# Feature-major products that stream both parts of the activations in one 512-column matmul, into two halves of a PSUM bank that are added afterwards

## The chip, the core and the metric

The kernel runs on one core of a Trainium2 chip. The metric is the device time in microseconds (us) of one execution. TensorE (PE in the profile) multiplies, VectorE (DVE) and ScalarE (ACT) evacuate PSUM and do the element-wise work, GpSimd (POOL) does a few small pieces, and SyncE (SP) issues the large loads; ScalarE issues some small ones.

## What is computed

Two transformer blocks over 256 tokens of width 1024, in float32. Cut to what matters:

```python
# first block
h = rmsnorm(x, g_mix);  z = h @ w_in            # x_rnn, g_rnn, q, k, v, gate_a, gate_b
y_a = (rg_lru(conv(x_rnn)) * gelu(g_rnn)) @ w_rnn_proj
y_b = sliding_window_attention(q, k, v) @ w_attn_proj
x = x + (sigmoid(gate_a) * y_a + sigmoid(gate_b) * y_b) @ w_out
x = x + square(relu(rmsnorm(x, g_mlp) @ w_up)) @ w_down      # w_up: 1024 x 4096
x = x + (p @ w_ple_proj) * sigmoid(rmsnorm(x, g_ple) @ w_ple_gate)
# second block
h = h + (g_a * (mla(...) @ w_attn_branch) + g_b * (pool(...) @ w_pool_branch)) @ w_mix_out
h = h + memory_cross_attention(rmsnorm(h), rmsnorm(mem))     # 4 heads of 256, 256 memory rows
h = h + moe(rmsnorm(h))                                      # 32 experts, two for each token
out = rmsnorm(h, final_norm_g)
```

## The kernel before

**Two parts of every operand.** TensorE takes a rounded form of float32 (float32r). So each weight and each activation is kept as a high part (a cast on ScalarE) and the rest (a subtraction on VectorE), made by `split` (L271 to L273), and each product is three matmuls into the same PSUM accumulator, leaving out rest times rest:

```python
def mm3(self, acc, xh, xl, wh, wl, start, stop):     # L304
    mm(acc, xh, wh, start=start, stop=False)         # L306
    mm(acc, xl, wh, start=False, stop=False)         # L307
    mm(acc, xh, wl, start=False, stop=stop)          # L308
```

**Two kinds of products.** `gemm` is token-major: 128 tokens of the activations are the stationary operand and up to 512 columns of weights stream. `gemm_fm` (L330) is feature-major: a block of 128 weight columns is stationary and the 256 tokens stream, so the result has features on the partitions. There the roles of the arguments of `mm3` are exchanged: L306 is high weight by high activation, L307 is the weight's rest by high activation, L308 is high weight by the activation's rest. One block is 8 steps over the 1024 inputs (k) of three matmuls each, 24 matmuls of 256 columns. Its result takes half of a PSUM bank, and a function `evac` reads it from there.

**Where feature-major products stand.** There are 64 such blocks: 16 at the start of the first block (`lru_in`, `gelu_in`, tile `acc`; their evacuation begins on VectorE with a multiplication by the norm's row, L710 and its twin in `gelu_in`), 32 in the MLP's up projection (`mlp`, tile `pt`; ScalarE's relu L860, VectorE's square L862, then a split into the tile `hid`), and 16 in the cross attention (keys and queries, tile `acc`, evacuated by a split). The activations of these products are `State` objects (`st`): for each part a tile of four k-steps by 256 tokens. `trans_split` fills a state four k-steps and 128 tokens at a time, 512 columns for each cast and subtraction.

**The order of the work.** The program is a list of parts. A part is a slice of weights that is split two parts ahead of its use (L272, L273 with the tiles `raw` and `w`), and the matmuls that use it. Background work (attention, recurrence) is advanced a step per part. A scheduler in the tile framework then orders each engine's instructions; each engine runs its own list in order. In the first block's first part the background is sliding-window attention: transposes of probabilities `pr` on TensorE (L464), copied by ScalarE to `pT` (L466), multiplied with the values (L841), heads turned by transposes (L817) that ScalarE casts to `qT` (L819); and the recurrence's gates (L719 on TensorE, L720 on ScalarE).

PSUM has four banks under the name `acc` and four under `pt`. Weights in flight and split weights share one pool of SBUF tiles.

Of the kernel before, what the change touches and what calls it, by code (L numbers as in the profile page):

```python
# [15 lines left out]
ALU = mybir.AluOpType  # L16
# [35 lines left out]
class Raw:  # L52
    """Weights on their way: loaded far ahead, in the order of use."""
# [5 lines left out]
class Part:  # L59
    """A slice of weights, split or as it is, and what runs on it."""  # L60
# [5 lines left out]
class State:  # L66
    """Activations, feature-major, as a float32r part and the exact rest: [128, kt, 256 tokens]."""

    def __init__(self, net, kt=8, early=False):
        self.net, self.kt, self.t = net, kt, {}  # L70
        self.new = net.early if early else net.act
        self.ss, self.r, self.rh = {}, {}, {}
# [5 lines left out]

    def v(self, i, kt, t=None, n=None):
        x = self._tile(i, kt // 4)  # L80
        c = slice(None) if t is None else slice(t * P, (t + 1) * P)
        return x[:, kt % 4, c] if n is None else x[:, kt % 4:kt % 4 + n, c]


class _Late:
    """A state that is made later."""
# [8 lines left out]
class Net:  # L95
# [28 lines left out]
    def early(self, shape, dt=F32, name="e"):  # L124
        """Tiles of the first block's first part only; their room then goes to weights on their way."""
# [36 lines left out]
    def later(self, n, fn):  # L162
        """Runs fn after n more parts."""
# [6 lines left out]
    def manual(self, engines=None):  # L170
        """From here on, the engines take their instructions in the order of the program."""
# [19 lines left out]
    def until(self, gens):  # L191
        """Advances the background until the generators of the list have ended."""
# [82 lines left out]
    def trans_gain(self, src, k0, n, gcol=None):  # L275
        """Transposes of src [128 tokens, n*128], n up to 4, scaled by a gain per feature."""
# [9 lines left out]
    def trans_split(self, srcs, st, k0, n, gcol=None):  # L286
        """Transposes and gains of each block of tokens of srcs, into the split state st."""
        xs = [(t, self.trans_gain(src, k0, n, gcol)) for t, src in srcs]
        for t, x in xs:
            self.split(x, st.v(0, k0, t, n), st.v(1, k0, t, n))  # L290

# [18 lines left out]
    def gemm(self, st, KT, w, c0, n, evac):  # L310
        """Token-major: out[t] = x[t] @ w[:, c0:c0+n]."""
# [18 lines left out]
    def gemm_fm(self, st, KT, w, c0, n, evac, space=None):  # L330
        """Feature-major: out[128 features, 256 tokens] for each block of 128 columns."""
        rs = [(k0, self.rawload(w, k0, min(4, KT - k0), c0, n)) for k0 in range(0, KT, 4)]
        for b in range(n // P):
            def fn(h, l, b=b):
                acc = (space or self.accp)()[:, 0:S]
                for k in range(KT):
                    self.mm3(acc, h[:, k, :], l[:, k, :], st.v(0, k), st.v(1, k), k == 0, k == KT - 1)
                evac(b, acc)
# [1329 lines left out]
```

## Time and profile before

| what | value |
|---|---|
| runs | 996.68, 992.30, 992.56 us; median 992.56 |
| span of the profiled execution | 990.5 us; the median of the runs is 2.06 us above it |
| TensorE busy | 965.8 us (98%) |
| VectorE busy | 555.0 us (56%) |
| ScalarE busy | 498.2 us (50%) |
| feature-major matmuls | 1536 of the 5445 on TensorE |

Busy time is time in which an engine has an instruction in it. Matmuls overlap: the next one starts before the one before it has left the array, so the mean duration of a row is longer than the distance from one start to the next. A clock column (PEclk) gives the granted TensorE clock as a share of full speed, 2.4 GHz.

### The profile page before, as it was taken

To read this page: it belongs to the slowest core of one execution; us is meant where nothing else is said; L and a number is where in the kernel's file an instruction comes from. 1 tells how busy PE (TensorE), PEld (TensorE's weight loads), DVE (VectorE), ACT (ScalarE), POOL (GpSimd) and SP (SyncE) were. 2 spreads that over 40 slices of the span, in tenths; PEclk is the share of its full clock that TensorE was granted. 3 is DMA by queue.
4 is the path that set the end of the run, shared out by engine and by line. 5 is a ranking of instruction groups with operands and counts; after the bars stand their busy time and mean duration, and the time that the engine had idled before them with its cause. 6 is when DMAs were issued, how large, how long until landed. Compare 5 with 4: busy or idle time off the path is not lost.

```text
span 990.5 us, 14266 instructions
## 1 busy us (share of the span) xinstructions
PE 965.8 (98%) x5445; PEld 740.2 (75%) x5445; DVE 555.0 (56%) x1102; ACT 498.2 (50%) x951; POOL 34.6 (3%) x67
## 2 busy tenths in 40 slices
PE   7999999999999999999999999999989999999995
PEld 5889888888999999889887878998854444444442
DVE  5987888777665555577655588664451212212112
ACT  5666799746654444466556646545333222323222
POOL 4200000000000000000100000000000000000000
PEclk9999999999999999999999999999989999999998
DMA  9553245574655555644663544446899999999981
GB/s 296 201 174 125 86 136 173 190 263 163 208 192 201 171 170 178 213 130 170 226 201 128 178 162 170 170 171 218 279 354 354 374 361 375 362 378 361 371 310 45
DMA packets 141317, 222.63 MB, mean 225 GB/s; under 512 B 9522, under 2 KB 79419, under 8 KB 139067
## 3 DMA queue, kind: packets, MB, share of 16 engines
q1 hardware_dynamic: 137552, 218.91, 64.9%
q10 hardware_dynamic: 3691, 2.74, 0.9%
q8 instruction: 45, 0.74, 0.3%
q14 instruction: 29, 0.24, 0.1%
HBM read 220.59 MB, written 1.05 MB: 224 GB/s over the span
## 4 chain that ended last, share of the span: by engine, by line
PE 94%; DVE 2%; ACT 1%; issue 1%; DMA 1%; POOL 0%; SPq 0%; DVEq 0%; POOLq 0%; ACTq 0%
PE acc L308 17%; PE acc L306 17%; PE acc L307 17%; PE pt L1438 11%; PE pt L1459 6%; PE pt L1385 3%; PE acc L1469 3%; PE pt L307 3%; PE pt L308 3%; PE pt L306 3%; PE pt L279 1%; DVE w L273 1%; PE pt L464 1%; PE pt L1039 1%; PE pt L1451 1%
## 5 line engine op out<-in xcount | busy, mean ns | idle before, releaser
L273 DVE TENSOR_TENSOR w<-raw,w 128x512 fp32r<-128x512 f32 (+4 forms) x288 | 273.7, 969 | 114.9 <-ACT w L272 113.2
L272 ACT CAST w<-raw 128x512 fp32r<-128x512 f32 (+4 forms) x288 | 236.3, 847 | 153.8 <-PE acc L308 117.1
L306 PE MATMUL acc<-w,st 128*128 128x512 f32 (+2 forms) x508 | 197.7, 393 | 0.0
L307 PE MATMUL acc<-w,st 128*128 128x512 f32 (+2 forms) x508 | 197.5, 389 | 0.0
L308 PE MATMUL acc<-w,st 128*128 128x512 f32 (+2 forms) x508 | 193.4, 389 | 0.2 <-DVE w L273 0.2
L308 PEld LDWEIGHTS acc<-w,st 128*128 128x128 f32 x508 | 95.8, 189 | 19.0 <-DVE w L273 0.6
L306 PEld LDWEIGHTS acc<-w,st 128*128 128x128 f32 x508 | 95.9, 189 | 18.6 <-ACT st L272 0.5
L307 PEld LDWEIGHTS acc<-w,st 128*128 128x128 f32 x508 | 95.9, 189 | 17.6 <-DVE st L273 0.2
L273 DVE TENSOR_TENSOR y<-pt,y 128x512 fp32r<-128x512 f32 x32 | 22.1, 692 | 109.3 <-ACT y L272 109.3
L1438 PE MATMUL pt<-raw,xg 128*64 128x512 f32 x296 | 83.1, 598 | 0.0
L308 PE MATMUL acc<-st,w 128*128 128x256 f32 x256 | 73.7, 288 | 0.0
L306 PE MATMUL acc<-st,w 128*128 128x256 f32 x256 | 73.5, 287 | 0.0
L307 PE MATMUL pt<-st,w 128*128 128x256 f32 x256 | 72.4, 283 | 1.1 <-DVE w L273 1.1
L307 PE MATMUL acc<-st,w 128*128 128x256 f32 x256 | 73.4, 287 | 0.0
L306 PE MATMUL pt<-st,w 128*128 128x256 f32 x256 | 72.3, 283 | 0.0
L308 PE MATMUL pt<-st,w 128*128 128x256 f32 x256 | 71.8, 283 | 0.0
L1438 PE MATMUL pt<-rawa,xg 128*64 128x512 f32 x216 | 65.1, 598 | 0.0
L1438 PEld LDWEIGHTS pt<-raw,xg 128*64 128x64 f32 x296 | 24.7, 138 | 45.7 <-issue 44.8
L307 PEld LDWEIGHTS pt<-st,w 128*128 128x128 f32 x256 | 49.1, 192 | 1.5 <-DVE w L273 1.3
L306 PE MATMUL acc<-w,hid 128*128 128x512 f32 x128 | 50.0, 390 | 0.0
L307 PE MATMUL acc<-w,hid 128*128 128x512 f32 x128 | 49.9, 390 | 0.0
L308 PE MATMUL acc<-w,hid 128*128 128x512 f32 x128 | 49.8, 389 | 0.0
(361 smaller groups left out, 1460.5 us busy)
## 6 DMA issues: line engine op xcount, KB each, us to landing
raw<-in_w_in_dram SPq DMA_DIRECT2D x31, 1024.0 KB, 5.2
raw<-in_w_exp_gate_dram SPq DMA_DIRECT2D x37, 512.0 KB, 8.5
raw<-in_w_exp_up_dram SPq DMA_DIRECT2D x37, 512.0 KB, 8.7
raw<-in_w_exp_down_dram SPq DMA_DIRECT2D x17, 1024.0 KB, 9.5
raw<-in_w_up_dram SPq DMA_DIRECT2D x16, 1024.0 KB, 5.4
raw<-in_w_down_dram SPq DMA_DIRECT2D x16, 1024.0 KB, 6.8
rawa<-in_w_exp_down_dram SPq DMA_DIRECT2D x30, 512.0 KB, 8.1
rawa<-in_w_exp_gate_dram SPq DMA_DIRECT2D x54, 256.0 KB, 7.7
```

What stands on the lines that cost most here:

```text
L272: self.nc.scalar.copy(h, src)
L273: self.nc.vector.tensor_sub(l, src, h.bitcast(F32))
L279: self.nc.tensor.transpose(p[:, i, :], src[:, i * P:(i + 1) * P], self.ident)
L306: mm(acc, xh, wh, start=start, stop=False)
L307: mm(acc, xl, wh, start=False, stop=False)
L308: mm(acc, xh, wl, start=False, stop=stop)
L464: nc.tensor.transpose(p[:, i, :], pr[:, i, kb * P:(kb + 1) * P], self.ident)
L1039: nc.tensor.matmul(o, V[mb][:, c0:c0 + P], pT[h][:, mb, :], start=mb == 0, stop=mb == 1)
L1385: nc.tensor.matmul(p, xs[t][i][:, k * P:(k + 1) * P], oh[b, t].rearrange("p e s -> p (e s)"), start=n == 0, stop=n == 3)
L1438: nc.tensor.matmul(guP[p][64 * e:64 * e + 64], xg[b, hf][:, k, c0:c0 + 64], gu_of(tiles[e], k), start=kt == 0, stop=kt == 7)
L1459: nc.tensor.matmul(q[64 * e:64 * e + 64], hT[p][:, f, 64 * e:64 * e + 64], d_of(tiles[e], f, c), start=f == 0, stop=f == 1)
L1469: nc.tensor.matmul(acc[t, c], stt[b][:, j, t, :], y[p, c][i], start=False, stop=p == NP - 1 and i == 1)
```

## The change

`gemm_fm` issues two matmuls for each k-step instead of three. The weight's high part meets both parts of the activation at once, side by side, 512 columns into the two halves of one bank; the weight's rest meets the activation's high part, 256 columns, and is added into the first half. (At the last k-step the order of the two is turned round, so that the wide one closes both halves.) After the 16 matmuls ScalarE copies the second half to an SBUF tile `fm`, VectorE adds the first half to it, and `evac` reads `fm` in place of PSUM.

```diff
 class State:
-    def __init__(self, net, kt=8, early=False):
-        self.net, self.kt, self.t = net, kt, {}
+    def __init__(self, net, kt=8, early=False, both=False):
+        self.net, self.kt, self.t, self.both = net, kt, {}, both
...
+    def hl(self, kt):
+
+        if kt // 2 not in self.t:
+            self.t[kt // 2] = self.new([P, 2, 2, S], F32R, name="st")
+        return self.t[kt // 2][:, kt % 2]
+
     def v(self, i, kt, t=None, n=None):
+        c = slice(None) if t is None else slice(t * P, (t + 1) * P)
+        if self.both:
+            x = self.hl(kt)[:, i, c]
+            return x if n is None else self.t[kt // 2][:, kt % 2:kt % 2 + n, i, c]
...
-            self.split(x, st.v(0, k0, t, n), st.v(1, k0, t, n))
...
+            self.split_into(x, st, k0, t, n)
+
+    def split_into(self, x, st, k0, t, n):
+        m = 2 if st.both else n
+        for i in range(0, n, m):
+            self.split(x[:, i:i + m], st.v(0, k0 + i, t, m), st.v(1, k0 + i, t, m))
...
     def gemm_fm(self, st, KT, w, c0, n, evac, space=None):
...
-                acc = (space or self.accp)()[:, 0:S]
+                acc = (space or self.accp)((P, 2, S))
+                mm = self.nc.tensor.matmul
                 for k in range(KT):
-                    self.mm3(acc, h[:, k, :], l[:, k, :], st.v(0, k), st.v(1, k), k == 0, k == KT - 1)
-                evac(b, acc)
+                    last = k == KT - 1
+                    if last:
+                        mm(acc[:, 0], l[:, k, :], st.v(0, k), start=False, stop=False)
+                    mm(acc, h[:, k, :], st.hl(k), start=k == 0, stop=last)
+                    if not last:
+                        mm(acc[:, 0], l[:, k, :], st.v(0, k), start=False, stop=False)
+                s = self.act([P, S], name="fm")
+                self.nc.scalar.copy(s, acc[:, 1])
+                self.nc.vector.tensor_tensor(s, acc[:, 0], s, op=ALU.add)
+                evac(b, s)
...
-            xp = self.act([P, S], name="xp")
+            xp = acc
...
-            x = self.act([P, S], name="gx")
+            x = acc
...
-                r = self.act([P, S], name="r")
-                nc.scalar.activation(r, p, AF.Relu)
                 q = self.act([P, S], name="rq")
-                v.tensor_tensor(q, r, r, op=ALU.mult)
+                v.scalar_tensor_tensor(q, p, 0.0, p, op0=ALU.max, op1=ALU.mult)
```

The states that feed feature-major products (`st0`, the MLP's `st_u`, the cross attention's `st_x` and `st_mem`) are made with `both=True`. Their tiles hold two k-steps with both parts, so they are filled two k-steps at a time: two casts and two subtractions of 256 columns where there was one of 512. `lru_in` and `gelu_in` then work in place on `fm`; in the MLP, relu and square become one VectorE instruction (`scalar_tensor_tensor`), and ScalarE's relu is replaced by its copy.

On TensorE in the first part, where attention and recurrence run beside the feature-major blocks (of the blocks for `gelu_in`), this is before; the transposes L464 stand between the feature-major matmuls:

```order
L306 MATMUL acc<-st,w 128x256
L464 MATMUL pt<-ident,pr 128x128 x2
L307 MATMUL acc<-st,w 128x256
...
L464 MATMUL pt<-ident,pr 128x128 x6
L306 MATMUL acc<-st,w 128x256
...
L719 MATMUL pt<-xc,w_rg 128x256
L719 MATMUL pt<-xc,w_ig 128x256
L841 MATMUL pt<-pT,kv 64x256 x2
L817 MATMUL pt<-ident,qs 128x128 x4
L841 MATMUL pt<-pT,kv 64x256 x4
L817 MATMUL pt<-ident,qs 128x128 x4
```

and this after (L489 was L464, L745 was L719, L867 was L841, L843 was L817):

```order
L356 MATMUL acc<-st,w 128x256
L357 MATMUL acc<-st,w 128x512
L489 MATMUL pt<-ident,pr 128x128 x12
L745 MATMUL pt<-xc,w_rg 128x256
L745 MATMUL pt<-xc,w_ig 128x256
L867 MATMUL pt<-pT,kv 64x256 x2
L843 MATMUL pt<-ident,qs 128x128 x4
L867 MATMUL pt<-pT,kv 64x256 x4
L843 MATMUL pt<-ident,qs 128x128 x4
L745 MATMUL pt<-xc,w_rg 128x256
L745 MATMUL pt<-xc,w_ig 128x256
```

All twelve transposes have moved behind the feature-major matmuls, next to the products that need their copies.

On ScalarE at the same place, this is before (L735 and L737 belong to `gelu_in`, L713 to `lru_in`'s convolution, `st` and `qT` are the attention's output and turned heads):

```order
L713 ACTIVATE xc<-xp,cols 128x256 x3
L272 CAST w<-raw 128x512 x2
L466 COPY pT<-pt 128x512 x3
L272 CAST w<-raw 128x512 x2
L735 ACTIVATE gs<-gx 128x256
L272 CAST w<-raw 128x512 x4
L720 ACTIVATE r<-pt,hbb_rg 128x256
L720 ACTIVATE i<-pt,hbb_ig 128x256
L272 CAST st<-pt 128x2x128
L819 CAST qT<-pt 128x512
```

and this after (L739 was L713, L282 was L272, L491 was L466, L761 was L735, L746 was L720, L845 was L819; L361 is the new copy):

```order
L739 ACTIVATE xc<-fm,cols 128x256 x3
L282 CAST w<-raw 128x512 x6
L491 COPY pT<-pt 128x512 x3
L761 ACTIVATE gs<-fm 128x256
L746 ACTIVATE r<-pt,hbb_rg 128x256
L746 ACTIVATE i<-pt,hbb_ig 128x256
L282 CAST st<-pt 128x2x128
L845 CAST qT<-pt 128x512
L361 COPY fm<-acc 128x256
L282 CAST st<-pt 128x2x128
L845 CAST qT<-pt 128x512
```

The casts of weights that stood between the copies `pT` and the gate `r` now stand ahead of the copies.

On VectorE at the beginning of the MLP, from the instruction that takes the norm's factor (L386, in the change L411) on, this is before. `w_2703` is the weights of the fifth block of the up projection, two halves of 512 columns; `hid` is a split of a finished block:

```order
L386 TENSOR_SCALAR s_2611<-s_2609 128x1
L862 TENSOR_TENSOR rq_2647<-r_2645 128x256
L273 TENSOR_TENSOR w_2703<-raw_2404,w_2703 128x512
L273 TENSOR_TENSOR w_2703<-raw_2450,w_2703 128x512
L273 TENSOR_TENSOR hid_2644<-rq_2647,hid_2643 128x256
L862 TENSOR_TENSOR rq_2683<-r_2681 128x256
```

and this after, where `w_2609` is the fifth block's weights, `w_2761` the eighth's, `w_2794` the first of the down projection, L362 the new addition and L886 relu and square in one:

```order
L411 TENSOR_SCALAR s_2531<-s_2529 128x1
L362 TENSOR_TENSOR fm_2555<-pt_2538,fm_2555 128x256
L886 SCALAR_TENSOR_TENSOR rq_2560<-fm_2555 128x256
L283 TENSOR_TENSOR w_2609<-raw_2316,w_2609 128x512
L283 TENSOR_TENSOR w_2609<-raw_2362,w_2609 128x512
...
L283 TENSOR_TENSOR w_2761<-raw_2316,w_2761 128x512
L283 TENSOR_TENSOR w_2761<-raw_2362,w_2761 128x512
L362 TENSOR_TENSOR fm_2631<-pt_2614,fm_2631 128x256
L960 TENSOR_SCALAR s_2602<-s_2602 128x16
L283 TENSOR_TENSOR w_2794<-raw_2426,w_2794 128x1024
```

One more 256-column instruction stands between the norm's factor and the fifth block's weights.

## Rows read from the trace of the kernel before

**Rows 1.** The page's span, busy time of the engines, and chain by engine.

```profile
span 990.5 us, 14266 instructions
PE 965.8 (98%) x5445; PEld 740.2 (75%) x5445; DVE 555.0 (56%) x1102; ACT 498.2 (50%) x951; POOL 34.6 (3%) x67
PE 94%; DVE 2%; ACT 1%; issue 1%; DMA 1%; POOL 0%; SPq 0%; DVEq 0%; POOLq 0%; ACTq 0%
```

**Rows 2.** Groups by shape: feature-major matmuls, two of six; busy us, mean ns.

```profile
L308 PE MATMUL acc<-st,w 128*128 128x256 f32 x256 | 73.7, 288 | 0.0
L306 PE MATMUL pt<-st,w 128*128 128x256 f32 x256 | 72.3, 283 | 0.0
```

**Rows 3.** TensorE's timeline in the MLP: start us, duration us.

```profile
248.07 0.28 PE L306 MATMUL pt<-st,w 128*128 128x256 f32 x1
...
250.95 0.28 PE L306 MATMUL pt<-st,w 128*128 128x256 f32 x1
...
270.95 0.39 PE L306 MATMUL acc<-w,hid 128*128 128x512 f32 x1
...
274.80 0.39 PE L308 MATMUL acc<-w,hid 128*128 128x512 f32 x1
...
280.24 0.39 PE L308 MATMUL acc<-w,hid 128*128 128x512 f32 x1
280.47 0.28 PE L306 MATMUL pt<-st,w 128*128 128x256 f32 x1
```

**Rows 4.** Groups by shape: ScalarE and VectorE on 256 columns.

```profile
L862 DVE TENSOR_TENSOR rq<-r 128x256 f32<-128x256 f32 x32 | 13.6, 425 | 14.9 <-ACT r L860 14.9
L860 ACT ACTIVATE r<-pt 128x256 f32<-128x256 f32 x32 | 12.3, 384 | 38.1 <-PE pt L308 38.1
```

**Rows 5.** VectorE's timeline: three evacuations in a row, and two subtractions of 512 columns.

```profile
119.94 1.08 DVE L710 TENSOR_TENSOR xp<-acc,rrow 128x256 f32<-128x256 f32 x3
...
257.33 1.29 DVE L273 TENSOR_TENSOR w<-raw,w 128x512 fp32r<-128x512 f32 x2
```

**Rows 6.** Stretches: length, busy us of PE, PEld, DVE, ACT, POOL; PEclk, DMA share, GB/s.

```profile
70.00:143.00 73.00, 71.93 (x581) 66.06 (x580) 56.30 (x148) 54.42 (x148) 0.00 (x0) 1.00 0.38 131
245.00:269.50 24.50, 23.41 (x196) 23.21 (x195) 16.73 (x45) 15.11 (x34) 1.88 (x4) 1.00 0.50 165
347.70:359.30 11.60, 11.60 (x98) 11.57 (x97) 7.08 (x11) 6.01 (x11) 0.00 (x0) 1.00 0.68 223
609.00:656.00 47.00, 47.00 (x394) 46.96 (x393) 30.71 (x56) 24.31 (x50) 1.73 (x2) 1.00 0.52 188
```

**Rows 7.** TensorE's timeline at the start: a wait for split weights.

```profile
18.40 0.50 PE L308 MATMUL acc<-w,st 128*128 128x512 f32 x1 [0.21 <-DVE w L273]
```

**Rows 8.** Timelines of ScalarE and TensorE around TensorE's wait in the attention stage.

```profile
113.89 2.17 ACT L272 CAST w<-raw 128x512 fp32r<-128x512 f32 x4
115.96 0.48 ACT L720 ACTIVATE r<-pt,hbb_rg 128x256 f32<-128x256 f32 x1
...
116.49 1.08 PE L841 MATMUL pt<-pT,kv 128*64 128x256 f32 x8 [1.07 <-ACT r L720]
...
167.76 1.57 ACT L466 COPY pT<-pt 128x512 f32<-128x512 f32 x3
```

**Rows 9.** Timelines of POOL, VectorE and TensorE at the beginning of the MLP.

```profile
255.57 0.82 POOL L1252 TENSOR_TENSOR wr<-wr,cols 128x32 f32<-128x32 f32 x2 [7.16 <-DMA wr<-in_w_router_dram]
256.93 0.15 DVE L386 TENSOR_SCALAR s<-s 128x1 f32<-128x1 f32 x1 [7.52 <-POOL s L349]
257.00 0.42 DVE L862 TENSOR_TENSOR rq<-r 128x256 f32<-128x256 f32 x1
256.71 0.28 PE L306 MATMUL pt<-st,w 128*128 128x256 f32 x1
258.07 0.38 PE L307 MATMUL pt<-st,w 128*128 128x256 f32 x1 [1.09 <-DVE w L273]
```

**Rows 10.** SyncE's queue: the first load of expert weights.

```profile
668.44 0.59 SPq L1356 DMA_DIRECT2D raw<-in_w_exp_gate_dram  x1
```

More of the change, by code (lines that the diff above doesn't have):

```diff
@@ L77, in _tile @@
         return self.t[i, j]
+    def hl(self, kt):
+        if kt // 2 not in self.t:
+            self.t[kt // 2] = self.new([P, 2, 2, S], F32R, name="st")
+        return self.t[kt // 2][:, kt % 2]
     def v(self, i, kt, t=None, n=None):
+        c = slice(None) if t is None else slice(t * P, (t + 1) * P)
+        if self.both:
+            x = self.hl(kt)[:, i, c]
+            return x if n is None else self.t[kt // 2][:, kt % 2:kt % 2 + n, i, c]
         x = self._tile(i, kt // 4)
-        c = slice(None) if t is None else slice(t * P, (t + 1) * P)
         return x[:, kt % 4, c] if n is None else x[:, kt % 4:kt % 4 + n, c]
@@ L612, in first @@
         def first():
-            self.split(x0, st.v(0, 0, 0, 4), st.v(1, 0, 0, 4))
+            self.split_into(x0, st, 0, 0, 4)
             self.trans_split([(1, part(0, 1))], st, 0, 4, g)
@@ L645, in block1 @@
         w_in = a["w_in"][0]
-        st = self.st0 = State(self, early=True)
+        st = self.st0 = State(self, early=True, both=True)
         self.step(self.start)
-        st_r, st_a, st_m, st_u, st_g, st_2 = (State(self) for _ in range(6))
+        st_r, st_a, st_m, st_g, st_2 = (State(self) for _ in range(5))
+        st_u = State(self, both=True)
         KV, Q = {}, {}
@@ L958, in block2 @@
         st_q, st_kv, st_at, st_po = State(self, 3), State(self, 2), State(self, 4), State(self, 4)
-        st_m, st_x, st_o, st_f = (State(self) for _ in range(4))
+        st_m, st_o = (State(self) for _ in range(2))
+        st_x = State(self, both=True)
         g1 = []
@@ L1003, in block2 @@
         mem = []
-        self.st_mem = State(self)
+        self.st_mem = State(self, both=True)
         self.step(lambda: mem.append(self.background(self.memory())))
```

## The prediction

> **What bounds the kernel now.** I read the page first. TensorE is busy for 965.8 of 990.5 us, and the chain that ended last is TensorE for 94% of the span; VectorE is in it for 2%, ScalarE for 1% [rows 1]. So time is saved only by shortening TensorE's own list, and it is lost wherever TensorE comes to stand. Then I looked at what a feature-major matmul costs. The groups give a mean of 283 to 288 ns, in six groups of 256 [rows 2], and a reader may be tempted to price the change by them: three at 285 against one wide at 390 and one narrow at 285 would save 180 ns for each of 512 k-steps, 92 us. That is wrong, as the timeline shows. From the matmul at 248.07 to the one at 250.95 there are 24 of them, all starting at even distances: 2.88 us, 120 ns from start to start. From 270.95 to 274.80 there are 17 of 512 columns: 226 ns each [rows 3]. The rest of a duration lies under the next matmul. The difference, 106.5 ns for 256 more columns, is one column for each cycle of 2.4 GHz, and 13.5 ns are left that a matmul costs whatever its width. Last I read the stretches with feature-major blocks, to see how much room the two evacuating engines have, and the few places where TensorE waits.
>
> **What is removed on TensorE.** A k-step was three starts of 120 ns, 360. It becomes 226 + 120 = 346: the same 768 columns, one fixed part less. A narrow matmul behind a wide one starts after 0.23 us (280.24 to 280.47), which is a wide one's own distance, so alternating widths cost nothing extra [rows 3]. 64 blocks of 8 steps make 512 steps, 512 x 13.5 ns = 6.9 us: 1.7 in the first stage, 3.5 in the MLP, 1.7 in the cross attention. A block goes from 2.88 to 2.77 us. The clock has nothing to give: the granted clock is 1.00, the upper of its levels at 2.4 GHz, in each of these stretches [rows 6].
>
> A page of the Trainium skill, "TensorE: Matmul & The Clock Gate", section "Back-to-back issue gap", has N / 2.4 + 2.5 ns for an isolated matmul of N columns; by that the fixed part would be 2.5 ns and the change would save 512 x 2.5 ns = 1.3 us, an estimate. The same section gives some 131 ns for 512 columns in a stream of weight loads and matmuls, which the 226 ns of this trace do not bear out. This kernel's own spacing decides.
>
> **What is added on the other engines.** For each block ScalarE gets a copy of 256 columns out of PSUM and VectorE an addition. ScalarE's relu of that shape takes 384 ns, and VectorE's square 425 [rows 4]; three VectorE evacuations in a row took 1.08 us, so one more moves the queue by (1.08 - 0.42) / 2 = 0.33 us [rows 4, 5]. In the MLP the copy takes the relu's place, so only VectorE gains work: four blocks, 1.3 us in a stretch of 11.60 with 7.08 busy; it comes to 8.4 of about 11.2 [rows 6], still a quarter free, and the addition hides there. The cross attention's 16 blocks bring VectorE from 30.71 to 36.0 and ScalarE from 24.31 to 30.4, of 47 less 1.7 [rows 6]: hidden too, at most 0.8 us for the last block's evacuation. The first stage is the full one: VectorE goes from 56.30 to 61.6 and ScalarE from 54.42 to 60.5, of 73 less 1.7 [rows 6]. On the mean that fits, but there attention needs ScalarE in time.
>
> The halved splits cost little: two pieces of 256 columns move VectorE's queue by 0.66 us, one of 512 by at most 1.29 / 2 = 0.65 [rows 5]. At the start TensorE already waits 0.21 us for split weights that stand behind such splits [rows 7]: I take +0.2, bounds 0 and 0.5. A wide matmul also needs the activation's rest at once, where L306 and L307 could go ahead of it; at the MLP's first block that leaves next to nothing spare, and I count up to 0.3 in the range.
>
> **The attention stage.** Before, TensorE loses 1.07 us at 116.49, waiting for ScalarE's `r`, which stands behind four casts of weights (2.17 us) [rows 8]. In the new order the casts stand ahead of the copies `pT`, and the transposes come all after the feature-major matmuls that used to lie between them. So three copies (1.57 us [rows 8]) and behind them `gs`, `r`, `i`, `st`, `qT` (five pieces of about 0.38 [rows 4]), 3.5 us of ScalarE, meet a TensorE that has only small pieces to do: the last eight transposes, two gates and four turns, at 0.12 us or less some 1.7 us. 1.8 us stand, 1.07 of them in place of the old wait: +0.7. The stage has four such groups of copies; I count this twice, +1.5. Bounds: -1.1, if the old wait goes and no other comes, and +6.1, if all sixteen copies of 0.38 us come onto TensorE's path. I stay near the lower end, since the whole stretch of 73 us shows barely 1.1 us of TensorE idle though ScalarE is 75% busy [rows 6].
>
> **The MLP's beginning.** Here VectorE stands 7.52 us for the norm's factor from POOL, which itself waits 7.16 us for the router's weights [rows 9], a load that ScalarE's queue issues. TensorE meanwhile does four blocks and stands at the fifth, whose weights VectorE splits only after it resumes: 256.71 to 258.07, 1.09 us idle [rows 9]. The resume at 256.93 is set by the load, not by TensorE. After it the new order has one more 256-column piece ahead of those weights: +0.33. TensorE's four blocks end 4 x 0.11 = 0.43 us sooner, which is only waited away. And the load's issue stands behind halved casts on ScalarE: up to +0.4. That makes 1.2. Next late are the down projection's first weights, behind the eighth block's. By then VectorE has done two additions, two `rq`, one `hid` and eight pieces of weights (four blocks'), 5 x 0.33 + 8 x 0.65 = 6.9 us after 256.93; a cast twice 512 wide on ScalarE, 2 x 2.17 / 4 = 1.1 us [rows 8], may have to follow. TensorE is there after 1.4 + 2 x 2.77 = 6.9 us, so it stands up to 1.1 us if the cast needs the buffer that this split frees: I take 0.5. Together +1.7, bounds 0.3 and 3.
>
> **The cross attention's first block** waits for its state's rest and for one more copy on ScalarE: +0.3, bounds 0 and 0.8 (0.38 + 0.42 [rows 4]). What is saved before 668.44 counts in full: SyncE issues the first load of expert weights only there, when the products behind the last feature-major block are under way [rows 10], so the expert stage as a whole moves up.
>
> **Sum.** -6.9 + 0.2 + 1.5 + 1.7 + 0.3 = -3.2 us. On the profiled execution's span of 990.5 that gives 987.3; 2.06 us lie between that span and the median of the runs, 992.56, so **989.4**. What a measurement can tell from no change is about 0.5%, 5 us: 987.6 to 997.5.
>
> **Rivals.**
>
> *Nothing stalls that did not before.* For it: VectorE and ScalarE have a quarter free on the mean [rows 6]. Against it: the two places above. -6.9 + 0.2 gives 985.9; with the wait of 1.07 gone as well, 984.8. Faster.
>
> *The new copy and addition come onto TensorE's path in the first stage.* Place: the 16 blocks from 70 to 143, where the background's attention reads what ScalarE does in order behind each copy. Price: 0.38 + 0.42 = 0.8 us for each block [rows 4], 12.8 for all: -6.9 + 0.2 + 12.8 + 1.7 + 0.3 gives 1000.7. It is slower by over 0.5% once all stalls reach 11.9, so once 12 of the 16 blocks pay. For it: ScalarE at 85% of that stretch, an engine that goes in order, and work that runs on into the stretch behind. Against it: four banks of `acc` let TensorE go on for three blocks, 8 us, before an evacuation holds it.
>
> *There is no fixed part to save.* Then three matmuls and two cost the same, and the stalls remain: +3.7, 996.3. The even 120 ns over 24 starts and 226 over 17 speak against it [rows 3]. By the 2.5 ns that the Trainium skill gives in the section named above, the time would be 995.0.
>
> **Chances.** My forecast, where stalls take 2 to 10 of the 6.9 us: 0.52, of which 0.03 lies below 987.6. The first rival 0.26, the second 0.17, the third 0.05. So faster 0.29, within 0.5% 0.54, slower 0.17. The range reaches from the first rival's best, 984.5, up to 998, short of the second's full price, and leaves out about 2 in 10; the forecast's own range is 987 to 996.
>
> **What would show it.** Starts in a block alternate by 226 and 120 ns and a block takes 2.77 us; if it takes 2.88, the third rival holds. The stretch of the cross attention shrinks by 1.4 to 1.7 us and that of four up blocks by 0.43. At the fifth up block the wait grows from 1.09 to about 2.2, and a wait of some 0.5 appears at the first down products. Between 70 and 180 TensorE's waits on ScalarE come to 2 to 4 us; over 9 would be the second rival. It goes wrong if the scheduler's other order opens a wait that I did not follow, above all in the attention stage.

## The result and the profile after

The changed kernel takes 999.52 us (median of 4 runs, 997.61 to 999.96), the kernel before 992.88 beside it. The ratio of the runs is 1.0057, 95% interval 1.0044 to 1.0069: slower by 0.57%, 5.7 us, where the two medians lie 6.6 us apart. The prediction had 989.4 and a range up to 998. The profiled execution is the fastest of the four, 997.61 us with a span of 995.9, so the traces show 5.4 us of it.

The page's first lines and chain after, to be read against [rows 1]:

```profile
span 995.9 us, 13347 instructions
PE 964.8 (97%) x4933; PEld 712.9 (72%) x4933; DVE 578.4 (58%) x1182; ACT 510.7 (51%) x999; POOL 33.5 (3%) x67
PE 90%; DVE 5%; ACT 2%; issue 1%; DMA 1%; POOL 0%; SPq 0%; DVEq 0%; POOLq 0%; ACTq 0%
```

TensorE has 512 instructions fewer, yet its share of the chain falls from 94% to 90%, and VectorE's rises from 2% to 5%: the end is now held up by VectorE in places. Where, is seen by laying a few starts from TensorE's timeline side by side. First the kernel before: first and last feature-major matmul of the first stage, first and last of the MLP, first and last feature-major one of the cross attention (start us, duration us).

```profile
70.47 0.39 PE L306 MATMUL acc<-st,w 128*128 128x256 f32 x1
...
141.91 0.28 PE L308 MATMUL acc<-st,w 128*128 128x256 f32 x1
...
245.11 0.36 PE L306 MATMUL pt<-st,w 128*128 128x256 f32 x1
...
426.52 0.39 PE L308 MATMUL acc<-w,hid 128*128 128x512 f32 x1
...
609.16 0.28 PE L306 MATMUL acc<-st,w 128*128 128x256 f32 x1
...
655.97 0.28 PE L308 MATMUL acc<-st,w 128*128 128x256 f32 x1
```

And the same six places after:

```profile
70.65 0.50 PE L357 MATMUL acc<-st,w 128*128 128x512 f32 x1
...
139.90 0.40 PE L357 MATMUL acc<-st,w 128*128 128x512 f32 x1
...
250.53 0.48 PE L357 MATMUL pt<-st,w 128*128 128x512 f32 x1
...
432.72 0.39 PE L323 MATMUL acc<-w,hid 128*128 128x512 f32 x1
...
615.40 0.39 PE L357 MATMUL acc<-st,w 128*128 128x512 f32 x1
...
661.12 0.40 PE L357 MATMUL acc<-st,w 128*128 128x512 f32 x1
```

The start is 0.18 us later. The 16 blocks of the first stage run 2.2 us shorter (71.44 to 69.25), but what stands between them and the MLP grows by 7.4 (103.20 to 110.63). The MLP grows by 0.8 (181.41 to 182.19). The cross attention shrinks by 1.1 (46.81 to 45.72). Together +5.1; at the last matmul of all the kernel is 5.3 us later, the remaining 0.2 arising between these stages and behind them.

TensorE's waits after (us in total, times, longest); those of the start, the routing and the experts and those under 0.5 us are left out:

```profile
PE pt L489 <- DVE pr L481: 3.5, 1, 3.5
...
PE pt L357 <- DVE fm L362: 1.9, 1, 1.9
...
PE pt L359 <- DVE w L283: 0.5, 1, 0.5
PE pt L745 <- ACT qT L845: 0.5, 1, 0.5
```

The first stands behind the blocks of the first stage, where TensorE had not waited before; among those blocks its idle time is 1.05 us, where it was 1.07 before [rows 8]. The second and third are at the fifth up block, where it had lost 1.09 [rows 9].

**The attention stage.** The fourth group of softmax probabilities `pr`, before: ScalarE takes their exponentials from 158.59 on, VectorE makes the probabilities from 161.43 on, and TensorE's transposes start at 165.58 without a wait.

```profile
158.59 0.49 ACT L445 ACTIVATE pr<-pt,s 128x256 f32<-128x256 f32 x1
...
161.43 1.93 DVE L456 TENSOR_SCALAR pr<-pr,s 128x128 f32<-128x128 f32 x8
...
165.58 0.60 PE L464 MATMUL pt<-ident,pr 128*128 128x128 f32 x4
```

After, on ScalarE, VectorE and TensorE (the idle time and what ended it stand in brackets):

```profile
161.90 1.06 ACT L282 CAST w<-raw 128x1024 fp32r<-128x1024 f32 x1 [0.30 <-PE acc L323]
162.86 0.47 ACT L470 ACTIVATE pr<-pt,s 128x256 f32<-128x256 f32 x1
...
163.56 2.35 DVE L283 TENSOR_TENSOR w<-raw,w 128x1024 fp32r<-128x1024 f32 x2
165.83 1.09 DVE L764 SCALAR_TENSOR_TENSOR g<-gs,fm 128x256 f32<-128x256 f32 x3
...
167.40 1.19 DVE L283 TENSOR_TENSOR st<-t,st 128x1024 fp32r<-128x1024 f32 x1
168.60 1.89 DVE L481 TENSOR_SCALAR pr<-pr,s 128x128 f32<-128x128 f32 x8
...
169.00 1.51 PE L489 MATMUL pt<-ident,pr 128*128 128x128 f32 x6 [3.47 <-DVE pr L481]
```

The exponentials stand behind a cast of weights that itself waits for TensorE to give a buffer back, and the probabilities behind weights, gelu's `g` and a state. They are 7.2 us later than before, the exponentials 4.3. There had been 2.2 us of slack (the probabilities ended at 163.36, the transposes began at 165.58), and TensorE is there at the same time as before, at 165.53.

**The MLP's beginning**, on POOL, VectorE and TensorE:

```profile
261.76 0.82 POOL L1277 TENSOR_TENSOR wr<-wr,cols 128x32 f32<-128x32 f32 x2 [7.62 <-DMA wr<-in_w_router_dram]
...
263.12 0.15 DVE L411 TENSOR_SCALAR s<-s 128x1 f32<-128x1 f32 x1 [8.18 <-POOL s L374]
263.19 0.42 DVE L362 TENSOR_TENSOR fm<-pt,fm 128x256 f32<-128x256 f32 x1
...
263.76 0.47 PE L357 MATMUL pt<-st,w 128*128 128x512 f32 x1 [1.86 <-DVE fm L362]
264.73 0.58 PE L359 MATMUL pt<-st,w 128*128 128x256 f32 x1 [0.50 <-DVE w L283]
```

VectorE stands for the norm's factor as before, but now the first block's addition (L362) stands behind it. The four `pt` banks are taken, so the fifth block cannot begin at all. Before, ScalarE's relu had read a bank out by then, and the block began and waited for weights at its second matmul. Both long waits cost something further, which the stretches show (length, busy us of PE, PEld, DVE, ACT, POOL; granted clock, DMA share, GB/s):

```profile
264.60:267.90 3.30, 3.17 (x10) 2.79 (x11) 3.30 (x9) 1.21 (x3) 0.00 (x0) 0.50 0.00 0
...
169.00:172.00 3.00, 3.00 (x11) 2.46 (x12) 2.63 (x8) 3.00 (x8) 0.00 (x0) 0.50 0.02 5
172.00:173.00 1.00, 1.00 (x5) 0.83 (x4) 0.00 (x0) 1.00 (x3) 0.00 (x0) 0.82 0.00 0
```

Behind each, TensorE works at a granted clock of 0.50, which is 1.2 GHz, for about 3.4 us: in the first stage from 169.00 on, and in the microsecond behind 172.00, with its mean of 0.82, for another 0.36. Half of that time is lost, some 1.7 us each.

The first stage as a whole, before and after, in the same columns:

```profile
70.47:245.11 174.64, 173.57 (x1065) 150.30 (x1065) 135.67 (x262) 123.95 (x259) 0.00 (x0) 1.00 0.49 168
...
70.65:250.53 179.88, 175.36 (x938) 143.32 (x937) 140.43 (x280) 128.49 (x276) 0.00 (x0) 0.99 0.48 163
```

TensorE's idle time, length less busy time, goes from 1.07 to 4.52 us. Its busy time less the 1.7 us that the clock takes is 173.7 us; before it was 173.6. So the 5.2 us by which the stage grew are 3.5 of waits and 1.7 of the lower clock, and nothing of what the matmuls should save can be seen.

### The profile page after: what moved, and what is told of

Its sections match the earlier page's. It is cut to its first block, busy times and chain, and to the rows that moved or that the text cites. A ratio compares the mean times of both kernels' runs of the same rounds, so it can differ in the third digit from the quotient of the medians.

```text
span 995.9 us, 13347 instructions
## 1 busy us (share of the span) xinstructions
PE 964.8 (97%) x4933; PEld 712.9 (72%) x4933; DVE 578.4 (58%) x1182; ACT 510.7 (51%) x999; POOL 33.5 (3%) x67
## 3 DMA queue, kind: packets, MB, share of 16 engines
HBM read 220.59 MB, written 1.05 MB: 223 GB/s over the span
## 4 chain that ended last, share of the span: by engine, by line
PE 90%; DVE 5%; ACT 2%; issue 1%; DMA 1%; POOL 0%; SPq 0%; DVEq 0%; POOLq 0%; ACTq 0%
PE acc L323 14%; PE acc L321 14%; PE acc L322 14%; PE pt L1463 11%; PE pt L1484 6%; PE acc L357 5%; PE pt L357 5%; PE pt L1410 3%; PE acc L1494 3%; PE acc L359 2%; PE pt L359 2%; DVE w L283 2%; PE pt L289 1%; PE pt L489 1%; DMA x<-in_x_dram 1%
## 5 line engine op out<-in xcount | busy, mean ns | idle before, releaser
L282 ACT CAST w<-raw 128x512 fp32r<-128x512 f32 (+4 forms) x288 | 236.5, 848 | 156.3 <-PE acc L323 112.6
L357 PE MATMUL pt<-st,w 128*128 128x512 f32 x256 | 90.7, 402 | 1.9 <-DVE fm L362 1.9
L357 PE MATMUL acc<-st,w 128*128 128x512 f32 x256 | 89.8, 401 | 0.0
L359 PE MATMUL pt<-st,w 128*128 128x256 f32 x224 | 63.7, 284 | 0.5 <-DVE w L283 0.5
L359 PE MATMUL acc<-st,w 128*128 128x256 f32 x224 | 64.0, 286 | 0.0
L357 PEld LDWEIGHTS acc<-st,w 128*128 128x128 f32 x256 | 46.2, 188 | 8.3 <-ACT gate L448 0.2
L1470 DVE SCALAR_TENSOR_TENSOR th<-th,pt 128x256 f32<-128x256 f32 x16 | 6.7, 421 | 75.6 <-ACT th L1469 75.6
```

What stands on the lines that cost most here:

```text
L282: self.nc.scalar.copy(h, src)
L357: mm(acc, h[:, k, :], st.hl(k), start=k == 0, stop=last)
L359: mm(acc[:, 0], l[:, k, :], st.v(0, k), start=False, stop=False)
```

## The experiments

Each was timed beside the kernel before; ratios are to that one. The table's stages come from TensorE's timeline in the same way as above: from the first feature-major block to the MLP's first matmul, from there to its last, and the cross attention's blocks. They are those of one profiled execution of each kernel, which lies up to 2.5 us from its kernel's median (e9).

| kernel | ratio, 95% interval | first stage us | MLP us | cross att. us |
|---|---|---|---|---|
| before | 1 | 174.64 | 181.41 | 46.81 |
| changed | 1.0057 (1.0044 to 1.0069) | 179.88 | 182.19 | 45.72 |
| e1 first stage only | 1.0055 (1.0041 to 1.0069) | 180.24 | 181.76 | 46.81 |
| e2 MLP only | 0.9997 (0.9986 to 1.0008) | 174.63 | 180.61 | 46.81 |
| e3 cross attention only | 0.9995 (0.9986 to 1.0004) | 174.64 | 181.71 | 45.72 |
| e4 changed, early load | 1.0013 (1.0004 to 1.0022) | 180.05 | 177.87 | 45.72 |
| e5 three narrow, added | 1.0116 (1.0096 to 1.0135) | 183.73 | 182.36 | 46.82 |
| e6 wide, nothing added | 1.0014 (1.0005 to 1.0024) | 176.54 | 181.46 | 45.72 |
| e7 before, early load | 0.9987 (0.9978 to 0.9996) | 174.64 | 180.08 | 46.81 |
| e8 MLP and cross att., early load | 0.9962 (0.9950 to 0.9975) | 174.63 | 177.87 | 45.72 |
| e9 as e4, 24 parts | 1.0054 (1.0041 to 1.0067) | 182.76 | 177.87 | 45.72 |
| e10 as e7, 24 parts | 1.0044 (1.0031 to 1.0057) | 178.75 | 180.08 | 46.81 |
| e11 as e8, 24 parts | 1.0014 (1.0005 to 1.0023) | 180.36 | 177.87 | 45.70 |
| e12 as e4, first stage lru_in only | 1.0019 (1.0010 to 1.0028) | 179.90 | 177.87 | 45.69 |
| e13 as e4, gelu's product on POOL | 1.0042 (1.0028 to 1.0055) | 183.07 | 177.88 | 45.72 |
| e14 as e7, gelu's product on POOL | 0.9989 (0.9980 to 0.9998) | 176.02 | 180.08 | 46.82 |
| e15 as e4, addition on POOL | 1.0066 (1.0052 to 1.0079) | 184.69 | 177.88 | 45.69 |
| e16 as e7, first stage two products | 0.9994 (0.9985 to 1.0003) | 175.13 | 180.08 | 46.81 |
| e17 as e4, first stage gelu_in only | 0.9992 (0.9983 to 1.0001) | 179.21 | 177.87 | 45.72 |
| e18 as e4, copy on VectorE | 1.0028 (1.0017 to 1.0039) | 181.46 | 177.88 | 45.72 |

**Which stage (e1, e2, e3).** Each run changes one group of blocks; the other states are made without `both=True` and keep the old product and evacuation:

```diff
+                if not st.both:
+                    acc = (space or self.accp)()[:, 0:S]
+                    for k in range(KT):
+                        self.mm3(acc, h[:, k, :], l[:, k, :], st.v(0, k), st.v(1, k), k == 0, k == KT - 1)
+                    evac(b, acc)
+                    return
```

> Only the first stage's 16 blocks (lru_in, gelu_in, state st0) get the wide matmul, copy and addition; MLP and cross attention as before. Theory A (the change's loss sits in two places, most of it in the first stage, where softmax pieces come late on ScalarE and VectorE and TensorE then runs at the lower clock for some us): about +5 us against before, the MLP reached 5 us later. Theory B (copy and addition cost every one of the 64 blocks the same): a quarter of the whole loss, +1.3 us. Theory C (it is the MLP's beginning that costs, and the first stage is neutral): -1 to +1 us.

> Only the MLP's 32 blocks are changed. Theory A: a wait of about 2 us at the fifth up block for the bank that the addition must free, then a stretch at the lower clock, against 3.5 us saved on matmuls: +0.5 to +1 us against before. Theory B: half of the whole loss, +2.7 us. Theory C: +4 us or more.

> Only the cross attention's 16 blocks are changed. Theory A: no new wait there, so 1.7 us of matmuls less some tenths: -1.1 us against before. Theory B: +1.3 us. Theory C: -1.1 us.

e1 has the whole loss (+5.5 us). The MLP and the cross attention change little (their intervals hold 1). A cost spread evenly over the blocks (B) is out, and so is C, which left the first stage neutral. Theory A is right on the place, but not on e2: it had +0.5 to +1 us with a stretch at the lower clock, and e2 came at -0.3 (interval -1.4 to +0.8), its MLP 0.8 us shorter than before. The wait came, the lower clock did not (the last line is a stretch, in the columns used above; its clock is 1.00):

```profile
258.23 0.47 PE L363 MATMUL pt<-st,w 128*128 128x512 f32 x1 [1.73 <-DVE fm L368]
259.20 0.39 PE L365 MATMUL pt<-st,w 128*128 128x256 f32 x1 [0.49 <-DVE w L283]
...
258.20:263.20 5.00, 4.47 (x24) 3.70 (x25) 5.00 (x13) 2.77 (x5) 0.00 (x0) 1.00 0.01 2
```

**The router's load (e4, e7, e8).** The load of the router's weights is issued some 80 us earlier (at 175.75 in e4, at 252.40 in the changed kernel):

```diff
 def embed_in(self):
     self.st_p = State(self, 2)
+    self.wr0 = self.act([P, 8, 36], name="wr0")
+    self.nc.scalar.dma_start(self.wr0, self.a["w_router"].rearrange("(k p) n -> p k n", p=P))
```

> The changed kernel with the load of the router's weights issued some 70 us earlier, from another buffer, so that POOL need not wait for it when the norm's factor of the MLP is due. If the MLP's loss comes from VectorE standing behind that factor with the first addition, by which a PSUM bank stays taken: the wait of 1.86 us at the fifth up block, the 0.5 us behind it and the stretch at the lower clock go, about 4 us less than the changed kernel, +1 to +2 us against before. Rival: the wait is for the split of the fifth block's weights, which the load does not hold: the wait moves to that and no more than 1 us is won.

> The kernel before, with the load of the router's weights issued early, as in the run of the changed kernel with that edit. It has the wait of 1.09 us at the fifth up block, and no stretch at the lower clock there: -1 to -1.5 us against before. If the early load does harm or good elsewhere, other than at the MLP's beginning, this run shows it: outside -2 to 0.

> The change in the MLP and the cross attention alone, the first stage as before, and the router's load early. By the sum of what was measured apart: -0.3 (MLP) -0.5 (cross attention) -4.3 (early load) = -5.1 us against before, and by the trace's matmuls and waits -3.5 -1.1 -1.3 = -5.9. Rival, that the pieces do not add because the next wait takes what one wins: -3 us or less.

In e4 the wait at the fifth block is gone, and so is the slow stretch; TensorE is busy throughout, at a clock of 1.00:

```profile
250.40:270.00 19.60, 19.60 (x114) 17.16 (x113) 14.71 (x39) 12.10 (x28) 1.29 (x2) 1.00 0.43 146
```

The MLP takes 177.87 instead of 182.19, 4.3 us less. In the kernel before the same edit wins 1.3 in the MLP. So the one wait cost 4.3 us with the change and 1.3 without it; with the MLP changed but no stretch at the lower clock it is 2.7 (180.61 in e2 against 177.87 in e8). e8 is the fastest kernel of the study: 988.37 us, 3.8 less than before by the ratio, of which the early load alone makes 1.3 (e7). It fell short of the sum of -5.1, because that sum counted 4.3 for the early load, the lower clock included, which e2 did not have; with 2.7 it is -3.5.

**Added work or shorter TensorE (e5, e6).** e5 keeps the added work without the wide matmul, e6 the reverse:

```diff
 e5:
-                    mm(acc, h[:, k, :], st.hl(k), start=k == 0, stop=last)
+                    mm(acc[:, 0], h[:, k, :], st.v(0, k), start=k == 0, stop=False)
+                    mm(acc[:, 0], l[:, k, :], st.v(0, k), start=False, stop=False)
+                    mm(acc[:, 1], h[:, k, :], st.v(1, k), start=False, stop=last)
 e6:
-                s = self.act([P, S], name="fm")
-                self.nc.scalar.copy(s, acc[:, 1])
-                self.nc.vector.tensor_tensor(s, acc[:, 0], s, op=ALU.add)
-                evac(b, s)
+                evac(b, acc[:, 0])
```

> All 64 blocks with the new states, halves, copy and addition, but three matmuls of 256 columns for a k-step as before (the activation's rest into the second half of the bank), so TensorE saves nothing. If the loss comes from the copy and addition on ScalarE and VectorE, it is here too, and the 6.9 us of the matmuls are not made: +8 to +12 us against before. Rival, that the wide matmul itself or TensorE's new list is at fault: 0 to +2 us.

> The wide matmul of the change in all 64 blocks, but evacuation as before, from the first half alone; copy and addition are left out, and with them the product of the weights' high part and the activations' rest. If copy and addition make the loss, what remains is the saving on TensorE: -5 to -7 us against before, the first stage without the wait of 3.5 us for the probabilities. Rival, that the shorter TensorE list or the halved splits bring the waits: 0 to +5 us.

e5 came as expected if copy and addition make the loss (+11.6 us by the ratio). e6 did not: with nothing added and TensorE's list shorter, the first stage still takes 1.9 us longer than before, and the MLP no less. The first stage of e6:

```profile
69.92:246.46 176.54, 173.61 (x937) 142.49 (x937) 135.22 (x264) 124.18 (x260) 0.00 (x0) 1.00 0.48 166
```

TensorE is idle for 2.93 us there, 1.9 more than before, at a clock of 1.00, and busy for as long as before. The halved splits are in e6 as well; VectorE's and ScalarE's busy times are those of the kernel before to within half a microsecond, but no run has the splits alone, so whether they or TensorE's shorter list bring these waits is open. In e6's MLP the fifth block waits for its weights, as long as the changed kernel waited for the bank:

```profile
259.93 0.38 PE L359 MATMUL pt<-st,w 128*128 128x256 f32 x1 [1.86 <-DVE w L283]
```

So there, too, it is VectorE's late resume that costs, and the bank only takes the place of the weights.

**Softmax earlier (e9, e10, e11).** The background is advanced two steps a part for longer:

```diff
-    FAST = 18
+    FAST = 24
```

> The changed kernel with the router's load early and, besides, the attention and recurrence in the background advanced two steps a part for the first 24 parts instead of 18, which puts the last softmax pieces ahead of the gelu blocks' evacuation in the lists of ScalarE and VectorE; no instruction is added or taken away. If the first stage loses by the place of these pieces: the wait of 3.5 us for the probabilities goes, and the stretch at the lower clock behind it; -3 to -6 us against before (the same without this edit was +1.3). Rival, that ScalarE and VectorE simply have too much to do in that stage: the wait moves elsewhere and the time stays at 0 to +2.

> The kernel before with the same two edits (router's load early, 24 parts), as a control for the place of the background work: it had only one wait of 1.07 us in that stage, so -1.5 (early load) and up to -1.3 more: -1.5 to -3 us against before. If it gains as much as the changed kernel does, the edit says nothing on the change.

> As the run with only the MLP and the cross attention changed and the router's load early, with 24 parts. Against the changed kernel with these two edits it tells what the wide matmuls of the first stage are worth when nothing waits there: it should be 1 to 2 us slower than that one (1.7 us of matmuls), -4 to -6 us against before. Rival: the copy and addition of the first stage cost more than its matmuls save, and this one is the faster.

My theory that the fourth group's place alone makes the loss fell, and e9 (+5.4 us) and e10 (+4.4) missed their expectations. The fourth group's wait went, but others came among the blocks, in the kernel before as well (+4.1 us in e10's stage). The edit moves other pieces of the background too, so it does not test that place by itself. Of the other waits in e9, one is:

```profile
143.16 0.66 PE L489 MATMUL pt<-ident,pr 128*128 128x128 f32 x4 [1.77 <-ACT r L746]
```

e11 was faster than e9 by 2.4 us in that stage (4.0 by the ratios), not slower: the first stage's copy and addition cost more than its matmuls save under this order too.

**How much of the added work (e12, e17).** In one, `gelu_in` keeps three narrow matmuls and its old evacuation (`wide=False`), in the other `lru_in`.

> The changed kernel with the router's load early, and in the first stage only the eight blocks of lru_in with the wide matmul, copy and addition; gelu_in's eight blocks have three narrow matmuls and the evacuation from PSUM as before. Half of the added work of that stage is gone, but in VectorE's list the last softmax pieces still stand behind gelu's evacuation. If the place makes the loss: +1 to +3 us against before, with the wait for the probabilities about as it was. If the amount of work makes it: -1 to -2 us, with the wait halved or gone.

> The changed kernel with the router's load early, where in the first stage only gelu_in's eight blocks have the wide matmul, copy and addition, and lru_in's are as before. With lru_in's alone it was +1.9 us against before, with both +1.3, with none -3.8. If each half's work counted by itself, this would be about -4 (what the other half leaves of the sum). If any of it makes the softmax pieces late, +1 to +3 again. If the place of the pieces by the scheduler decides by chance, anything between -5 and +3.

In the profiled executions the stage loses 5.3 us with lru_in alone, 4.6 with gelu_in alone, 5.4 with both, and 1.9 with all wide matmuls and nothing added (e6). By the ratios, against e8, which has the first stage as before, it is 5.7 with lru_in alone, 3.0 with gelu_in alone and 5.1 with both. The two accounts differ for e17: its profiled execution has a stretch at the lower clock behind these waits (mean clock 0.991), while nine of its eleven executions show 0.993 or 0.994. So the work does not count by its amount, since lru_in's half brings as much as both; of gelu_in's half that is not shown. e12 (+1.9 us) came as expected if the place of the softmax pieces decides; e17 (-0.8) fits only the wide range that was given for chance. e12's transposes still wait 2.92 us for the fourth probabilities, e17's 0.92 and 1.22.

**Which engine sets the pace (e13 to e16, e18).** In e13 and e14 the last product of each gelu block goes to POOL, in e15 the 16 additions (ScalarE then copies both halves), in e18 the 16 copies to VectorE, and e16 takes one product of three away:

```diff
 e13, e14:
-            v.scalar_tensor_tensor(r["g"][:, b, :], s, 1.0, x, op0=ALU.add, op1=ALU.mult)
+            nc.gpsimd.tensor_scalar(s, s, 1.0, None, op0=ALU.add)
+            nc.gpsimd.tensor_tensor(r["g"][:, b, :], s, x, op=ALU.mult)
 e15, first stage:
+                    self.nc.scalar.copy(s2, acc)
+                    self.nc.gpsimd.tensor_tensor(s, s2[:, 0], s2[:, 1], op=ALU.add)
 e16, first stage:
+                        self.nc.tensor.matmul(acc, h[:, k, :], st.v(0, k), start=k == 0, stop=False)
+                        self.nc.tensor.matmul(acc, l[:, k, :], st.v(0, k), start=False, stop=k == KT - 1)
 e18, first stage:
-                self.nc.scalar.copy(s, acc[:, 1])
+                self.nc.vector.tensor_copy(s, acc[:, 1])
```

> The changed kernel with the router's load early, and gelu's last multiplication of each block (8 of them, 0.33 us each on VectorE) done by POOL in two instructions. If VectorE's load sets the pace behind the blocks: the wait for the probabilities falls by about 2.7 us and with it the stretch at the lower clock, -2 to -4 us against before (without the edit +1.3). If the place of the softmax pieces decides: within 1 us of +1.3.

> Control: the kernel before with the same two edits. TensorE hardly waits in that stage there, so the relief should win nothing beyond the -1.5 us of the early load: -1 to -2.5 us against before.

> The changed kernel with the router's load early; in the first stage ScalarE copies both halves (512 columns) and POOL adds them, so VectorE has none of the 16 additions (5.3 us) and ScalarE 16 x 0.2 us more. If VectorE's load sets the pace: -2 to -5 us against before. If ScalarE's does, or the length of the evacuation's chain: 0 to +3 us.

> The kernel before with the router's load early, where the 16 blocks of the first stage leave out the third product (high weight by the activation's rest, L308): 128 matmuls of 0.12 us, 15.4 us less on TensorE, all other work the same. If ScalarE and VectorE set the pace of that stage, TensorE cannot have it: -2 to -7 us against before, the rest comes back as waits. If TensorE sets it: -15 to -17 us.

> The changed kernel with the router's load early; in the first stage VectorE makes the copy of the second half as well as the addition, so ScalarE has as much to do as in the kernel before and VectorE 16 x 0.33 us more than in the change. If ScalarE's queue sets the pace there: -4 to -1 us against before. If VectorE's does: +4 to +8 us.

e16 is the plainest: 15.4 us of matmuls less on TensorE, and the stage is 0.5 us longer than in e7. TensorE waits instead (in total, times, longest), and the last line is that stage as a whole, in the columns used above:

```profile
PE pt L468 <- DVE pr L460: 5.0, 2, 4.1
...
PE pt L723 <- DVE w L273: 2.2, 1, 2.2
PE pt L723 <- ACT pT L470: 1.8, 1, 1.8
PE pt L723 <- ACT pr L449: 1.5, 2, 1.2
...
70.77:245.90 175.13, 164.64 (x938) 136.87 (x937) 135.17 (x262) 124.72 (x259) 0.82 (x2) 0.96 0.50 168
```

The idle time is 10.5 us, 9.4 more than in the kernel before, and the mean clock of 0.96 over 175 us takes some 7 more. Without the lower clock the stage might have been shorter; that is not shown.

The fourth probabilities come at 164.93 there, 4.6 us later than in e7 (1.4 of them because the stage began later), though VectorE and ScalarE have the same work, in another order:

```profile
164.93 1.92 DVE L460 TENSOR_SCALAR pr<-pr,s 128x128 f32<-128x128 f32 x8
```

and in e7:

```profile
160.37 1.92 DVE L456 TENSOR_SCALAR pr<-pr,s 128x128 f32<-128x128 f32 x8
```

Taking work off VectorE by way of POOL made the stage longer, by 3.0 us in e13 and 4.6 in e15 over e4, and by 1.4 in the control e14. POOL takes 1.31 and 0.85 us for the two pieces that replace one of 0.42 on VectorE, and 0.91 for an addition. Copies on VectorE (e18) add 1.4 over e4. No expectation of a relief came true: e13, e15, e16 and e18 lie outside every range that was given for them.

## Why the prediction was wrong

**The first step that failed is the one on the attention stage, and in it the way I counted.** I took the 1.7 us of matmuls there as saved and added 1.5 for waits that I could follow in the new order. Measured, the stage lost 5.2: 3.5 of waits, 1.7 of the lower clock. The waits that I had followed, on ScalarE's copies among the blocks, did not come: idle time there is 1.05 us, and between 70 and 180 TensorE waits for ScalarE for 0.5 us, not 2 to 4. The wait of 3.47 us stands behind the blocks and is for VectorE. The fault lies in the sentence "I stay near the lower end, since the whole stretch of 73 us shows barely 1.1 us of TensorE idle though ScalarE is 75% busy". TensorE's small idle time does not show that the other engines have room. In e16 TensorE loses 15.4 us of work there and the stage does not get shorter. TensorE and the attention's way through ScalarE and VectorE ended nearly together, 2.2 us apart at the fourth group. I did not ask for that distance, nor look behind the blocks, where the loss is. With it, what is saved on TensorE beyond that distance does not count, and probabilities that come more than 2.2 us later make TensorE wait.

**The second step that failed is "The clock has nothing to give", a term put at nothing.** I read the granted clock of 1.00 before and did not ask what the new waits would do to it. The two stretches at 0.50 cost 1.7 us each, 3.4 of the 5.3 us. In the prediction's own terms: the attention stage lost 5.2 where +1.5 stood, with none of the 1.7 us of matmuls to set against it; the other matmuls brought -3.3 instead of -5.2; and the MLP's beginning cost +3.0 instead of +1.7.

Of the 5.2 us, e6 shows 1.9 with the wide matmuls and halved splits alone, all of it waits, and e4 some 3.5 more with copies and additions, half of it the lower clock. Whether each of these is the amount of work or the order that the scheduler makes of it, I could not settle. e16's later probabilities with unchanged evacuation speak for the order; e12, where half of the work costs as much as all of it, agrees. But e16's edit changes what TensorE delivers as well as the order, and in e9 to e11 the one other order that was tried moved the waits and kept the loss.

**The matmul term was mis-sized**: -6.9 predicted; -3.3 measured in the MLP and the cross attention, where 5.2 were predicted, and nothing in the first stage. Where nothing waits, the MLP goes from 180.08 (e7) to 177.87 (e4), 2.21 us in 256 steps, and the cross attention by 1.09 in 128: 8.6 ns a step, not 13.5. At that rate the first stage's 128 steps would be 1.1 us, which its busy time does not show. TensorE's timeline after, start and end of the MLP's second block first, then part of a later one:

```profile
253.39 0.39 PE L357 MATMUL pt<-st,w 128*128 128x512 f32 x1
...
256.16 0.39 PE L357 MATMUL pt<-st,w 128*128 128x512 f32 x1
...
269.19 0.40 PE L357 MATMUL pt<-st,w 128*128 128x512 f32 x1
269.42 0.28 PE L359 MATMUL pt<-st,w 128*128 128x256 f32 x1
269.54 0.40 PE L357 MATMUL pt<-st,w 128*128 128x512 f32 x1
...
270.96 0.40 PE L357 MATMUL pt<-st,w 128*128 128x512 f32 x1
```

The second block takes 2.77 us, just what I had forecast. Later, five steps in 1.77 us are 354 ns a step, of which some 235 belong to the wide one, and most blocks take 2.81 to 2.82. I had taken 226 from a stretch of wide matmuls alone, and "alternating widths cost nothing extra" from a single pair [rows 3]; that holds for the MLP's first blocks and not for the later ones, and why is open. The rival without any fixed part is nevertheless out. By the 2.5 ns that the Trainium skill has for an isolated matmul ("TensorE: Matmul & The Clock Gate", "Back-to-back issue gap"), the MLP's 256 steps would save 0.6 us, an estimate. The 2.21 us measured there do not agree with it.

**The MLP's beginning**: +1.7 predicted, +3.0 measured (4.3 against 1.3 before, by e4 and e7). The place and the cause behind it, VectorE standing for a factor that waits for the router's load, were right. What was late next was the bank and not the weights; the size was off because I had not thought of the clock: the waits at the fifth block, 2.36 us, are near the 2.2 that I had, in part by luck, since the load itself took 0.6 us longer to land after its issue (252.40 to 261.76, before 246.80 to 255.57) and in e3, whose MLP is unchanged, the wait is 1.38. The wait at the first down products, 0.5, did not come.

**Right**: no new wait in the cross attention; and that everything before the experts counts in full (from the last feature-major matmul to the last matmul of all it is 324.55 us before and 324.67 after). The start (+0.18, +0.2 predicted) proves nothing: in kernels with the first stage as before, its first block starts anywhere between 69.41 us (e7) and 70.50 (e2).

**The rival that put the copy and addition on TensorE's path** gave 1000.7, close to what came, by another way: no block of the first stage is held up by its evacuation, the blocks run 2.2 us shorter. An addition held a bank only at the MLP's fifth block.

## What to carry to other kernels

A TensorE that is 98% busy may still be within two microseconds of what other engines allow. Before counting a saving on it, take some of its work away in each stage and see whether the time follows; where it does not, the stage belongs to the chain through the other engines, or to the order that the scheduler makes of their lists, and work added there may cost more than its duration. Count a stretch at the lower clock behind a long wait, too, as a possible price. For a PSUM bank, ask which instruction frees it and what stands ahead of that one in its engine's list: a late, unrelated load can hold it. And a stage-by-stage trial can keep the part of a change that pays, as e8 does.

## What the runs showed of the hardware

- Behind an idle time of 1.86 and 0.50 us close together, and behind one of 3.47 us, TensorE's granted clock was 0.50 (1.2 GHz) for about 3.4 us; in e6, behind 1.86 us alone, it was 0.50 from 261.20 to 264.50. Behind 1.73 and 0.49 us in e2, and behind the 1.09 us of the kernel before [rows 6], it stayed at 1.00.
- Matmuls of 512 and 256 columns that alternate start 235 and 117 to 118 ns after one another in most blocks of the changed MLP, 352 to 354 ns for the pair, and 230 and 117 in its second and third block, where runs of one width gave 226 to 232 and 120.
- POOL took 0.91 us for an addition of two 128x256 tiles in SBUF (e15) and 1.31 for adding a constant to one (e13; 1.20 in e14), where VectorE did a piece of that shape in 0.42.
